# Two block products of seven parts in the output projection of a two-layer hybrid decoder trunk

## The chip, the cores and the metric

The kernel runs on one core of one Trainium2 chip. The metric is the device time in microseconds of one execution. The kernel before was run three times: 770.34, 770.36 and 770.64 us, median 770.36. Engines are called as the profile calls them: PE (TensorE matmul), PEld (its weight loads), DVE (VectorE), ACT (ScalarE), POOL (GpSimd), SP (SyncE, which here only issues DMAs).

## The reference

512 tokens and 16 learned meta tokens in front of them (528 in all) with 1024 features pass through two layers. All tensors are float32. Cut to what matters here, a layer computes:

```python
h = rmsnorm(h_res, norm_gain[l])
proj = h @ w_in[l]
u_pool, z_pool, c_q, c_kv, k_rope, z_mla, g_pool, g_mla = jnp.split(proj, IN_SPLIT_POINTS, axis=-1)
y_pool = (pool_mix(u_pool, ...) * jax.nn.silu(z_pool)) @ pool_w_up[l]
o_mla = mla(c_q, c_kv, k_rope, pos, ...)           # 8 heads, causal, latent queries and keys
y_mla = (o_mla * jax.nn.silu(z_mla)) @ mla_w_up[l]
merged = jax.nn.sigmoid(g_pool) * y_pool + jax.nn.sigmoid(g_mla) * y_mla
h_res = h_res + merged @ w_out[l]
```

After the second layer the meta tokens are dropped. The change is in the last line: `merged @ w_out[l]`, a product of 528 (in the second layer 512) tokens by 1024 by 1024.

## The kernel before, in words

Everything is held transposed: features lie on the 128 partitions, tokens along the free dimension. A product by a weight matrix is made output tile by output tile (128 features), over the tiles of the inner dimension K. To keep float32 accuracy, each operand is split into a high part rounded to float32r and a low part, the remainder, and each product is three matmuls in float32r, high by high, high by low and low by high (`mm3`, L181 to L183).

Weights come in chunks of four K tiles (128 x 512, 256 KB). `wload` (L170 to L178) fetches a chunk on SP's queue into one of three raw buffers, ACT rounds it to the high part `whi` (L176), DVE subtracts to get the low part `wlo` (L177). The high and low buffers rotate over three, or two, each.

The work is a plan of products (`Gemm`), filled by `register`, and one generator (`stream`) that emits them in order and loads one chunk ahead. `go` advances this generator and puts the other work (norm sums, pooling, heads) between its steps. This gives a program order with priorities; a scheduler then decides, from its own estimate of when each instruction is ready, the order in which each engine gets its instructions. On the chip each engine and each queue takes its instructions strictly in that order and waits on semaphores.

Tokens are worked in two halves of 264 in layer 0, and in one piece of 512 columns in layer 1, where meta tokens are no longer needed (its last output tile alone is made in two halves of 256). A PSUM buffer holds one tile of one such piece. There are four of the kind `mm` and three of the kind `S`.

The end of a layer runs through these products:

- mu0 to mu7, the MLA up-projection, four K tiles each. The evacuation `ev_mu` has DVE multiply PSUM with the gate (L980), POOL add the pool branch that lies in `xb[m]` (L982), and `split` round the sum on ACT into `hh[m]` (L275) and subtract on DVE into `hl[m]` (L276). These are the merged values, and the operand of the next product.
- o0 to o7, the output projection, eight K tiles each. The evacuation `ev_o` has DVE add the residual (L996), which SP fetched into a temporary tile, and store it. In layer 0 the result is the next layer's x, kept in `xb[m]`, squared on ACT and summed on POOL (`square_x`); in layer 1 it goes to the output `yT` (L1000).
- In layer 0, then, `split_h` of the next layer, which rounds x into the same `hh` and `hl` tiles that o0 to o7 read.

## Time and profile before

The profiled execution has a span of 768.5 us from the first to the last instruction. The execution's own time lies around that; the median of the runs, 770.36 us, is 1.86 us above the span.

| engine | busy, us | share of the span | instructions |
|---|---|---|---|
| PE | 763.8 | 99% | 5195 |
| PEld | 697.9 | 91% | 5195 |
| DVE | 544.1 | 71% | 1179 |
| ACT | 408.9 | 53% | 892 |
| POOL | 201.6 | 26% | 251 |

The granted PE clock is full (9 of 9 tenths) in all slices, and the DMA queues moved 84.05 MB, 109 GB/s on average.

How to read the profile's rows. A group of instructions is: line, engine, operation, output tile<-input tiles, shape, xcount | busy us, mean ns of one | idle time of the engine just before them, and what ended most of it. A row in order of time is: start us, duration us, engine, line, operation, tiles, shape, xcount [idle time before, and what ended it]. A row of the chain of work that ended last is: start, length, engine, tile, line. A row of waits is: who waited for whom, us in total, times, longest. A row of stretches is: stretch, its length, then the busy time of PE, PEld, DVE, ACT and POOL with counts, the granted clock, the share of the DMA engines' time and GB/s. A row of DMA issues ends in the size and the median time to landing. Durations of matmuls overlap, so the pace is read from starts.

### The profile page before, as it was taken

The page shows a single profiled execution, that of the slowest core. Times are in us where ns is not written, and L with a number is a line of the kernel's source. Part 1 is how long each engine was busy: PE and PEld are TensorE (multiplying, and loading weights), DVE is VectorE, ACT ScalarE, POOL GpSimd, SP SyncE. Part 2 cuts the span into 40 slices and gives each one's busy share as a digit, 9 for nine tenths or more (in the row PEclk, how much of TensorE's full clock was granted, in tenths as well). Part 3 has the DMA queues.
Part 4 walks back from the last instruction along what each step waited for, and adds up shares of the span by engine and source line. Part 5 has one row for each costly group of instructions (what it writes and reads, how often), then busy time and mean ns, then how long its engine had stood idle before and what let it go on. Part 6 is the DMA issues. An engine that isn't in the chain of part 4 may idle for free.

```text
span 768.5 us, 14355 instructions
## 1 busy us (share of the span) xinstructions
PE 763.8 (99%) x5195; PEld 697.9 (91%) x5195; DVE 544.1 (71%) x1179; ACT 408.9 (53%) x892; POOL 201.6 (26%) x251
## 2 busy tenths in 40 slices
PE   9999999999999999999999999999999999999998
PEld 9999999999999999999997898887888888888887
DVE  5588687357899977785376486773677989775842
ACT  6755656545556665634264355454446666664320
POOL 2026204012242233052220262040132434420500
PEclk9999999999999999999999999999999999999999
DMA  8533233343223222325642333334433332222372
GB/s 293 160 113 98 75 97 98 104 141 105 89 79 91 84 71 70 107 71 169 178 133 97 110 86 89 96 87 127 125 119 90 94 93 77 82 69 70 119 222 98
DMA packets 54931, 84.05 MB, mean 109 GB/s; under 512 B 10006, under 2 KB 18582, under 8 KB 54860
## 3 DMA queue, kind: packets, MB, share of 16 engines
q1 hardware_dynamic: 54716, 82.87, 35.6%
q8 instruction: 41, 0.67, 0.4%
q14 instruction: 30, 0.25, 0.1%
q10 hardware_dynamic: 144, 0.26, 0.1%
HBM read 76.69 MB, written 4.29 MB: 105 GB/s over the span
## 4 chain that ended last, share of the span: by engine, by line
PE 99%; DMA 0%; ACT 0%; DVE 0%; SPq 0%; issue 0%; ACTq 0%
PE mm L181 29%; PE mm L183 29%; PE mm L182 29%; PE mm L859 2%; PE S L181 2%; PE S L182 2%; PE S L183 2%; PE o L876 1%; PE o L872 1%; PE S L503 1%; PE S L470 0%; DMA xb<-xT 0%; PE S L806 0%; PE mm L922 0%; PE mm L395 0%; PE S L872 0%
## 5 line engine op out<-in xcount | busy, mean ns | idle before, releaser
L181 PE MATMUL mm<-hh,whi 128*128 128x264 f32 (+2 forms) x1080 | 339.9, 317 | 0.0
L182 PE MATMUL mm<-hl,whi 128*128 128x264 f32 (+2 forms) x1080 | 338.2, 314 | 0.0
L183 PE MATMUL mm<-hh,wlo 128*128 128x264 f32 (+2 forms) x1080 | 337.1, 315 | 0.0
L177 DVE TENSOR_TENSOR wlo<-raw,whi 128x512 fp32r<-128x512 f32 (+2 forms) x251 | 186.7, 748 | 98.6 <-ACT whi L176 94.6
L176 ACT ACTIVATE whi<-raw 128x512 fp32r<-128x512 f32 (+2 forms) x251 | 150.2, 602 | 181.3 <-PE mm L182 135.3
L181 PEld LDWEIGHTS mm<-hh,whi 128*128 128x128 f32 x1080 | 202.5, 188 | 12.9 <-ACT kp L474 0.4
L182 PEld LDWEIGHTS mm<-hl,whi 128*128 128x128 f32 x1080 | 203.0, 188 | 12.2
L183 PEld LDWEIGHTS mm<-hh,wlo 128*128 128x128 f32 x1080 | 201.9, 188 | 12.2
L743 POOL TENSOR_TENSOR tmp<-kp,bc 64x528 f32<-64x528 f32 x16 | 25.6, 1600 | 123.9 <-PE mm L183 70.0
L604 POOL TENSOR_TENSOR racc<-racc,tmp 128x264 f32<-128x264 f32 (+1 forms) x15 | 14.3, 956 | 133.1 <-ACT tmp L603 133.1
L832 POOL TENSOR_TENSOR pm<-pa,rs 128x16 f32<-128x16 f32 x32 | 9.1, 285 | 126.1 <-DVE rs L827 126.1
L982 POOL TENSOR_TENSOR tmp<-tmp,xb 128x264 f32<-128x264 f32 (+1 forms) x24 | 26.9, 1138 | 56.0 <-DVE tmp L980 55.9
L774 DVE CUSTOM_DVE_ANT_0 S<-S,maskw,nqs 128x400 f32<-128x400 f32 (+4 forms) x80 | 38.4, 499 | 4.4 <-PE S L183 4.0
L781 ACT ACTIVATE cq<-S,bia 128x400 f32<-128x400 f32 (+2 forms) x48 | 24.6, 516 | 27.1 <-DVE bia L774 18.1
L181 PE MATMUL mm<-u,whi 128*128 128x264 f32 (+1 forms) x108 | 34.7, 322 | 0.0
L181 PE MATMUL mm<-cq,whi 128*128 128x264 f32 (+1 forms) x108 | 34.7, 321 | 0.0
L183 PE MATMUL mm<-u,wlo 128*128 128x264 f32 (+1 forms) x108 | 34.7, 321 | 0.0
L183 PE MATMUL mm<-cq,wlo 128*128 128x264 f32 (+1 forms) x108 | 34.5, 321 | 0.0
L182 PE MATMUL mm<-cq,whi 128*128 128x264 f32 (+1 forms) x108 | 34.5, 321 | 0.0
L834 POOL TENSOR_TENSOR cq<-cq,rs 128x384 f32<-128x384 f32 (+1 forms) x32 | 32.8, 1024 | 0.0
L276 DVE TENSOR_TENSOR tl<-mm,th 128x384 fp32r<-128x384 f32 (+1 forms) x48 | 27.9, 596 | 5.0 <-ACT th L275 4.8
L275 ACT ACTIVATE th<-mm 128x384 fp32r<-128x384 f32 (+1 forms) x48 | 24.1, 523 | 10.2 <-PE mm L859 9.2
(270 smaller groups left out, 1378.6 us busy)
## 6 DMA issues: line engine op xcount, KB each, us to landing
raw<-win SPq DMA_DIRECT2D x143, 256.0 KB, 2.6
raw<-wout SPq DMA_DIRECT2D x32, 256.0 KB, 3.0
bc<-kdr SPq DMA_DIRECT2D x16, 264.0 KB, 3.6
raw<-wpu SPq DMA_DIRECT2D x16, 256.0 KB, 2.7
raw<-wmu SPq DMA_DIRECT2D x16, 256.0 KB, 2.7
raw<-wqb SPq DMA_DIRECT2D x12, 256.0 KB, 2.6
xb<-xT SPq DMA_DIRECT2D x8, 264.0 KB, 5.7
tmp<-xT SPq DMA_DIRECT2D x16, 132.0 KB, 3.4
```

Of the source, the lines that this page charges most:

```text
L176: act.activation(hi[:, :n], raw[:, :n], AF.Copy)
L177: dve.tensor_sub(lo[:, :n], raw[:, :n], hi[:, :n].bitcast(F32))
L181: first = pe.matmul(out, wh, xh, start=start, stop=False)
L182: pe.matmul(out, wh, xl, start=False, stop=False)
L183: newest[0] = pe.matmul(out, wl, xh, start=False, stop=stop)
L275: act.activation(hi[:, a:b], src, AF.Copy)
L276: return dve.tensor_sub(lo[:, a:b], src, hi[:, a:b].bitcast(F32))
L743: gp.tensor_mul(kf[r0:r0 + 64, :], self.kp[r0:r0 + 64, :], bc[r0:r0 + 64, :])]
L774: return dve.tensor_tensor_reduce(out=sv, in0=sv, in1=mask, scale=nqs[:, i, h:h + 1], scalar=3e38, op0=ALU.add, op1=ALU.min, accum_out=bia ...
L781: act.activation(pv, sv, AF.Exp, scale=-1.0, bias=bia[:, i:i + 1], accum_out=rs[:, c:c + 1])
L834: gp.tensor_mul(pt[i][:, NM:], pt[i][:, NM:], rs[:, i:i + 1].to_broadcast([P, n - NM]))
L982: gp.tensor_add(t[:, :b - a], t[:, :b - a], self.am[m][:, a:b])
```

## The change

In each layer o0 to o3 stay as they were. Tiles 4 to 7 become two pairs, (4, 5) and (6, 7). For a pair the weights form a 2 x 2 block matrix (two output tiles by two halves of K) and the merged values another (two halves of K by two halves of tokens, 264 or 256 columns each). Their product is formed by a scheme of seven block products in place of eight, each of four K tiles and three passes, 12 matmuls. It needs four sums of weight blocks and four sums of token blocks:

- weight sums, in DRAM buffers, made in the layer itself: SP copies four blocks per pair after `zp0`, and POOL issues DMAs that add further blocks to them (`weight_sums`, stages 1 to 3, after `zp3`, `cq5` and `qr1`);
- token sums (`combine_split`, 16 per layer, asked for after mu7): DVE adds or subtracts float32 blocks, ACT rounds the result to a high part, DVE takes the remainder. For that `ev_mu` now leaves the float32 sum in `xb[m]`; the buffers are those of the attention's values, keys and others that are free by then.

The loads of w_out go through a new function, `oload`, and run up to three chunks ahead in place of one (`deep`). It rotates over nine places for high and low parts, and uses three more raw buffers. For o1, o2 and o3 and for two of the seven parts of a pair, DVE's subtraction is replaced: ACT writes the negated high part into the low tile, and a DMA on POOL's queue adds the raw chunk to it.

The seven parts are accumulated in three PSUM tiles; after each part DVE adds what is there, times 0.5 or -0.5, to the residual row, which is now fetched as a whole ahead of the pair. One PSUM tile (B) goes on being accumulated over four parts, with such an add between any two of them. The x of o0 to o3 for the next layer moves from `xb[m]` to other tiles.

```diff
+PAIRS = (2, 3)
+PACE = 600.0
+DEEP = 2
+LOW = (3, 5)
...
+    def oload(j, src, by_dma):
+        if j % 2 == 1 and j > 5:
+            raw = slot(f"kn{j // 2 % 3}")
+        else:
+            raw = rawt()
+        fetch(src, 512, raw, sp)
+        kind = ("w", "t", "w", "cq0", "w", "cq2", "t", "q0", "q2")[j % 9]
...
+        act.activation(hi[:, :512], raw[:, :512], AF.Copy)
+        if by_dma:
+            act.activation(lo[:, :512], raw[:, :512], AF.Copy, scale=-1.0)
+            gp.dma_start(lo[:, :512].bitcast(F32), raw[:, :512], accum_op=ALU.add)
+        else:
+            dve.tensor_sub(lo[:, :512], raw[:, :512], hi[:, :512].bitcast(F32))
+        return hi, lo
...
+            if g_.operand is not None:
+                return g_.operand(c // 512)
+            if g_.deep:
+                j = (int(g_.name[1][1:]) * 2 + c // 512)
+                return oload(j, g_.src[:, c:c + 512], j > 1)
...
-            if i >= 3 and i + 1 < len(flat):
-                ahead.append(load(i + 1))
+            while made[0] < len(flat) and made[0] <= i + 1 + flat[made[0]][0].deep:
+                ahead.append(load(made[0]))
+                made[0] += 1
...
-                gp.tensor_add(t[:, :b - a], t[:, :b - a], self.am[m][:, a:b])
-                split(*self.mg[m], t[:, :b - a], a, b)
+                f = self.am[m][:, a:b]
+                gp.tensor_add(f, t[:, :b - a], f)
+                split(*self.mg[m], f, a, b)
...
+        def combine(self, w, k):
+            n = self.HV[0][1] - self.HV[0][0]
+            (a0, b0), (a1, b1) = self.HV
+            lo, hi = self.am[k], self.am[4 + k]
+            f = self.tf[w, k] = sqt()[:, :n]
+            eng = dve
+            if w == 1:
+                eng.tensor_sub(f, lo[:, a0:b0], lo[:, a1:b1])
+            elif w == 2:
+                eng.tensor_add(f, hi[:, a1:b1], self.tf[1, k])
+            elif w == 3:
+                eng.tensor_sub(f, hi[:, a1:b1], lo[:, a1:b1])
+            else:
+                eng.tensor_sub(f, self.tf[2, k], hi[:, a0:b0])
+
+        def combine_split(self, w, k):
+            self.combine(w, k)
...
+            sign = -1.0 if w == 2 else 1.0
+            act.activation(th, f, AF.Copy, scale=sign)
+            dve.scalar_tensor_tensor(out=tl, in0=f, scalar=sign, in1=th.bitcast(F32), op0=ALU.mult, op1=ALU.subtract)
+
+        def weight_sums(self, stage):
+            acc = lambda d, src: behind(gp.dma_start(d, src, accum_op=ALU.add, max_dma_last_dim=2048), newest[0])
+            for p in PAIRS:
+                w = lambda odd, c: wout[self.l, 2 * p + odd, :, 512 * c:512 * c + 512]
...
+                s1, s2, s3, s4 = self.ws[p]
+                if stage == 0:
+                    for d, src in ((s1, w(1, 0)), (s3, w(1, 0)), (s2, w(0, 0)), (s4, w(0, 1))):
+                        behind(sp.dma_start(d, src), newest[0])
+                elif stage == 1:
+                    acc(s1, w(1, 1))
+                    acc(s3, w(0, 0))
+                else:
+                    acc(*((s2, s1), (s4, s2))[stage - 2])
...
+                j = 4 * PAIRS[0] + 7 * (p - PAIRS[0]) + i
+                return oload(j, (raw(0, 0), raw(0, 1), s2, s1, s3, s4, raw(1, 1))[i], i in LOW)
...
+            def product(ps, w, xs, start):
+                for k in range(4):
+                    wh, wl = (x[:, k * P:(k + 1) * P] for x in w)
+                    xh, xl = xs[k]
+                    for j, (u, v) in enumerate(((wh, xh), (wh, xl), (wl, xh))):
+                        newest[0] = pe.matmul(ps, u, v, start=start and k == 0 and j == 0, stop=k == 3 and j == 2,
+                                              skip_group_check=not start)
...
+                if i == 0:
+                    product(B, w, quarter(0, a0, b0), True)
+                    add(m1, a0, b0, B, 0.5, False)
+                elif i == 1:
+                    product(A, w, quarter(4, a0, b0), True)
+                    add(m1, a0, b0, A, 0.5, True)
+                elif i == 2:
+                    product(B, w, ts(2), False)
+                    add(m1, a1, b1, B, 0.5, False)
...
-            for m in range(8):
-                add(f"o{m}", wout[l, m], D, evac=self.ev_o(m, nxt), xs=mg,
-                    segs=[(NM, NM + SEQ // 2), (NM + SEQ // 2, T)] if self.last and m == 7 else XS)
+            for m in range(2 * PAIRS[0]):
+                add(f"o{m}", wout[l, m], D, evac=self.ev_o(m, nxt), xs=mg, segs=XS)
+                plan[-1].deep = DEEP
...
+            for p in PAIRS:
+                add(f"o{2 * p + 1}", None, 7 * 512, body=self.pair_body(p, nxt))
+                plan[-1].operand, plan[-1].deep = self.pair_operand(p), DEEP
...
+            up("mu7")
+            flush()
+            for w in (1, 2, 3, 4):
+                for k in range(4):
+                    fill_now(PACE)
+                    self.combine_split(w, k)
             up("o7")
```

## The prediction

> **What bounds the kernel now.** I read the page's first part, then its chain of work, then stretches around the output projection, which is where the change sits.

> ```profile
> span 768.5 us, 14355 instructions
> PE 763.8 (99%) x5195; PEld 697.9 (91%) x5195; DVE 544.1 (71%) x1179; ACT 408.9 (53%) x892; POOL 201.6 (26%) x251
> PE 99%; DMA 0%; ACT 0%; DVE 0%; SPq 0%; issue 0%; ACTq 0%
> ```

> PE has no hole worth a word, and the chain that ended last is PE for 99% of its length. So a matmul taken away is time taken away, as long as nothing makes PE wait where it did not wait before. The last rows of the chain in time (765.13 below) are one add and one store, and they stay.

> The pace of a matmul is the step from start to start, not its own duration, because matmuls overlap:

> ```profile
> 346.07 0.29 PE L181 MATMUL mm<-hh,whi 128*128 128x264 f32 x1
> 347.54 0.28 PE L181 MATMUL mm<-hh,whi 128*128 128x264 f32 x1
> 351.81 0.28 PE L183 MATMUL S<-hh,wlo 128*128 128x264 f32 x1
> ...
> 720.38 0.39 PE L181 MATMUL mm<-hh,whi 128*128 128x512 f32 x1
> ...
> 754.63 0.39 PE L182 MATMUL mm<-hl,whi 128*128 128x512 f32 x1
> 759.02 0.40 PE L183 MATMUL mm<-hh,wlo 128*128 128x512 f32 x1
> 759.25 0.28 PE L181 MATMUL mm<-hh,whi 128*128 128x256 f32 x1
> ...
> 764.81 0.28 PE L183 MATMUL mm<-hh,wlo 128*128 128x256 f32 x1
> ```

> 346.07 to 351.81 is 47 steps, 0.122 us for 264 columns; 754.63 to 759.02 is 19 steps, 0.231 us for 512; 759.25 to 764.81 is 47 steps, 0.1183 us for 256. Also: the output projection of layer 0 starts at 346.07, its second half of tokens at 347.54, and that of layer 1 at 720.38. These are the handover points.

> VectorE at the handover from mu (the MLA up-projection) to o (the output projection), layer 0 then layer 1, as groups by form:

> ```profile
> L276 DVE TENSOR_TENSOR hl<-tmp,hh 128x264 fp32r<-128x264 f32 x16 | 11.3, 720 | 1.2 <-ACT hh L275 1.2
> L177 DVE TENSOR_TENSOR wlo<-raw,whi 128x512 fp32r<-128x512 f32 x7 | 5.5, 801 | 0.1
> L980 DVE SCALAR_TENSOR_TENSOR tmp<-cq,mm 128x264 f32<-128x264 f32 x12 | 4.8, 421 | 3.2 <-PE mm L183 3.0
> L982 POOL TENSOR_TENSOR tmp<-tmp,xb 128x264 f32<-128x264 f32 x16 | 14.6, 927 | 27.8 <-DVE tmp L980 27.6
> L176 ACT ACTIVATE whi<-raw 128x512 fp32r<-128x512 f32 x7 | 4.3, 622 | 4.5 <-PE mm L182 3.9 <-DMA raw<-wout 0.6
> ...
> L177 DVE TENSOR_TENSOR wlo<-raw,whi 128x512 fp32r<-128x512 f32 x10 | 10.2, 1032 | 0.9 <-ACT whi L176 0.9
> L276 DVE TENSOR_TENSOR hl<-tmp,hh 128x512 fp32r<-128x512 f32 x8 | 7.1, 905 | 1.1 <-ACT hh L275 1.1
> ```

> And the instructions themselves, in order of time (start, duration):

> ```profile
> 345.12 0.43 DVE L980 SCALAR_TENSOR_TENSOR tmp<-cq,mm 128x264 f32<-128x264 f32 x1
> 346.75 0.42 DVE L980 SCALAR_TENSOR_TENSOR tmp<-cq,mm 128x264 f32<-128x264 f32 x1
> 348.61 0.42 DVE L980 SCALAR_TENSOR_TENSOR tmp<-cq,mm 128x264 f32<-128x264 f32 x1
> 348.94 0.42 DVE L276 TENSOR_TENSOR hl<-tmp,hh 128x264 fp32r<-128x264 f32 x1
> 349.29 0.42 DVE L980 SCALAR_TENSOR_TENSOR tmp<-cq,mm 128x264 f32<-128x264 f32 x1
> ...
> 708.07 1.28 DVE L980 SCALAR_TENSOR_TENSOR tmp<-cq,mm 128x512 f32<-128x512 f32 x2 [2.86 <-PE mm L183]
> 721.71 1.87 DVE L980 SCALAR_TENSOR_TENSOR tmp<-cq,mm 128x512 f32<-128x512 f32 x3
> ```

> The idle columns are small after the first wait: VectorE is full there. An evacuation of mu6 runs at 346.75 and ends at 347.17; the matmul at 347.54 reuses that PSUM buffer. The margin is 0.37 us. VectorE's 71% over the whole span hides that it is within half a microsecond of being the bound at this place.

> **The change, part by part.**

> *Matmuls.* Of each layer the tiles 4 to 7 go from eight block products to seven. Layer 0 drops 24 matmuls of 264 columns: 24 x 0.122 = 2.93 us. Layer 1 drops 72 of 512 (16.63) and 24 x 2 = 48 of 256, and gets 168 of 256, so +120 x 0.1183 = 14.20: 2.44 us gained. Together -5.37 us, all on the path.

> *Token sums.* Per layer 16 VectorE sums, 16 ScalarE roundings, 16 VectorE remainders. The kernel's text asks for them after mu7, but in the changed program's instruction order they stand between the evacuations of mu, because their inputs are ready from mu0 on. Ahead of the mu6 evacuation named above stand nine token instructions that were not there, and two splits (hl) less; the weight subtractions (wlo) are five in both. One token instruction costs at least the step 348.61 to 348.94 to 349.29, 0.35 us, and at most what hl takes on average beside POOL, 0.72 less 0.08 of overlap, 0.64. A gain is excluded, since nothing is removed from that queue but the two splits. Seven net: 2.45 to 4.5 us. POOL's adds fill 14.6 of about 22 us, so I take 0.35 + 0.29 x 0.66 = 0.54, 3.8 us; less the margin, PE stands still 3.4 us (2.1 to 4.1) at the first o tile of layer 0.

> [...]

> *Layer 1.* From 708.07 on, VectorE must do, ahead of the remainder of the last mu tile: 8 evacuations (1.87/3 = 0.62) 5.0, 6 wlo (1.03 - 0.08) 5.7, 8 hl (0.905 - 0.08) 6.6, and 23 token instructions, 8.1 to 14.7, by 0.54 12.4. That is 25.4 to 32.0, taken as 29.7, so it is done at 737.8. PE needs it after 67 matmuls of its new order (60 of 512, 7 of 256): 720.38 + 14.7 = 735.1. Stall 2.7 us (0 to 4.6).

> *Weight parts.* 22 instead of 16 loads of w_out per layer: 6 x 0.62 on ACT more, and 10 negated copies, 6.2 us; VectorE's subtractions fall from 16 to 12. Ten low parts come from accumulating DMAs on POOL's queue. No row shows one. The nearest is a plain load of the same 256 KB:

> ```profile
> raw<-wout SPq DMA_DIRECT2D x32, 256.0 KB, 3.0
> ACT whi L176 <- PE mm L182: 135.3, 103, 3.9
> 346.00:392.00 46.00, 46.00 (x379) 46.00 (x379) 22.62 (x41) 17.86 (x32) 8.47 (x8) 1.00 0.59 174
> 765.13 0.42 DVE tmp L996
> 765.58 0.33 SPq L1000 DMA_DIRECT2D yT<-tmp  x1
> ```

> It reads one operand more, so 3.0 is the low end and 6.0, twice, the high one; I take 3.4, near the row, plus 0.9 on POOL to issue (its own add, 0.927; 0.3 as on SP would be the low end). Queued behind such a DMA on POOL are the last mu adds, behind their ScalarE copies the last roundings of mu, and behind them on SP the next load, which waits for the raw buffer that the DMA still reads. In layer 0: the fourth wlo of the stretch frees a raw buffer near 341.6, 12 us after the first evacuation by the counts above; its load takes 3.0 and three ScalarE items 0.62 each, so the copy for o1's second half ends near 346.4. Then +0.9 +3.4, the load that waits for that buffer +3.0, four ScalarE items 2.6: the last mu rounding ends at 356.3. PE wants it 58 matmuls in, 353.1, and with the 3.4 us it already stood still, 356.5: hidden, barely. Without that cover it is a stall of 3.2. In layer 1 the DMA for o1 starts behind the fifth mu add, near 720.5, and lands at 724.8 against 724.1; the load that reuses its buffer lands at 727.8, two ScalarE items and two issues on POOL later the DMA for o2 starts at 730.1 and lands at 733.5 against 731.6. Both hide under the 2.7.

> [...]

> *Sums of weights.* Per layer eight DRAM copies on SP in a row behind a zp matmul (8 x 0.33 = 2.6 us of SP) and eight accumulates on POOL. By 174 GB/s at a share of 0.59 the engines carry some 295 GB/s, so the 2.1 MB delay the next weight loads by about 7 us. The cover is the 135.3 us in which ScalarE waited for PE to release a weight buffer: loads stand two to three 2.9 us chunks ahead. Nothing, 0 to 3 us if that runs out. POOL's rope products and the last c_q sum wait behind accumulates by a few us; head 0 is some 30 us later.

> *Pair stage.* A part is 12 matmuls, 1.46 us. Per pair of 10.2 us VectorE has 5 wlo (0.69) and 7 adds (0.43), 6.5 us; ScalarE 9 x 0.62. The shared PSUM buffer is read by an add before the next part continues into it; in the new order some 20 matmuls, 2.4 us, lie between. Nothing; 16 x 0.43 if they touch. The DMA share of 0.59 rises by 6 loads and 10 accumulates: 16 to 26 times 256 KB at 295 GB/s, 14 to 23 of 46 us, to 0.9 or 1.1. Nothing at the low end.

> *The rest.* mu's sum is written in place (same add), the next layer's x moves to other buffers, residual rows load earlier, the last store is again 256 columns wide behind one add (765.13): nothing.

> Sum against the span: 768.5 - 5.37 + 3.4 + 2.7 = 769.2. The median of the runs, 770.36, is 1.86 above this execution's span: **771.1 us**. About 0.2% (1.5 us) is what a measurement of this kernel can tell from no change.

> **The rivals.**

> *Handover mostly holds (faster).* If a token instruction costs its bare 0.35 us, layer 0 stalls 2.1 and layer 1 not at all: 25.4 after 708.07 is 733.5, before 735.1. Sum -3.3: 767.1. For it: POOL's adds are a fixed amount of work, so their collisions need not grow with VectorE's. Against it: hl at 720 ns against 420 alone. It decides below about 0.45 us.

> *Accumulating DMAs bind (slower).* At 4.5 us each, layer 0's chain ends at 357.4 against 353.1, a stall of 4.3; in layer 1 the low part of o2 waits for two accumulates and a load in series, 736.0 against 731.6, 4.4: 773.7. At 6.0 us, 5.8 and 6.9: 777.7. I price it at 775.5. It decides from about 3.7 us. For it: the second read, and a DMA share near 1. Against it: loads on all 16 engines land in 3.0 with a share of 0.59.

> *It is hidden anyway.* If PE finds other work while a PSUM buffer is late: 765.0. Against it: PE takes its matmuls in the order written, and that order was set before any wait was known.

> **How the numbers follow.** Forecast, 0.38, own range 768.3 to 773: mostly inside 0.2%, a quarter slower. Handover holds, 0.33. DMAs bind, 0.25. Hidden, 0.04. Faster 0.30 + 0.04 + 0.03 = 0.37; the same 0.25 + 0.03 = 0.28; slower 0.35. The range 766.3 to 777.0 leaves out the hidden case and the worst DMAs, and because cases of both signs hold most of the chance it is wider than the forecast's own.

> **What would show it.** PE gaps at two places: the second half of o0 in layer 0, released by a VectorE evacuation, and near the last mu tile's remainder in layer 1. VectorE without idle from mu0 to o0, token instructions at 0.5 to 0.6 us. If PE's gaps are ended by a POOL-queue DMA instead, or landing takes over 4 us, the DMA rival holds. No gap anywhere and a PE time near 758 means it is hidden. I am wrong most simply if the gaps sit in the pair stage or behind the DRAM copies.

## The result, and the profile after

The changed kernel takes 784.63 us (median of four runs, 781.7 to 784.91) against 770.35: ratio 1.0173, 95% interval 1.0153 to 1.0192. The prediction was 771.1, range 766.3 to 777.0: the result lies outside it, on the slow side of every case in it (the slowest, DMAs of 6.0 us, gave 777.7). The profiled execution spans 782.8 us, 14.3 more than before.

The head of the page of the changed kernel, and its chain of work that ended last:

```profile
span 782.8 us, 14643 instructions
PE 767.4 (98%) x5219; PEld 699.5 (89%) x5219; DVE 571.8 (73%) x1250; ACT 433.5 (55%) x956; POOL 230.2 (29%) x287
...
PE 81%; DMA 10%; DVE 5%; issue 2%; ACT 1%; SPq 1%; POOL 0%; DVEq 0%; ACTq 0%; POOLq 0%
```

PE was 99% of the chain and is now 81%; a tenth of the chain is waiting for DMAs. PE's busy time went up although it has less to multiply, a first hint that some matmuls ran slower; the clock below shows it. PE's instructions in order of time, only those that waited longest (in brackets: the idle time and what ended it):

```profile
105.14 0.36 PE L208 MATMUL mm<-hh,whi 128*128 128x264 f32 x1 [0.61 <-DVE xb L585]
132.49 0.39 PE L210 MATMUL mm<-cq,wlo 128*128 128x264 f32 x1 [0.29 <-DVE wlo L179]
...
350.12 0.39 PE L208 MATMUL mm<-hh,whi 128*128 128x264 f32 x1 [2.03 <-DVE tmp L1016]
...
493.85 0.50 PE L208 MATMUL mm<-hh,whi 128*128 128x512 f32 x1 [0.32 <-ACT whi L178]
...
730.00 0.50 PE L208 MATMUL mm<-hh,whi 128*128 128x512 f32 x1 [0.44 <-DVE tmp L1016]
734.12 0.50 PE L210 MATMUL mm<-hh,tl 128*128 128x512 f32 x1 [1.07 <-DVE tl L199]
737.98 0.50 PE L209 MATMUL mm<-hl,th 128*128 128x512 f32 x1 [1.50 <-DVE hl L309]
...
762.32 0.80 PE L1099 MATMUL mm<-vt,th 128*128 128x256 f32 x2 [3.84 <-DVE bc L1105]
```

Such gaps lie in three parts of the program: the stretch where the weights are summed (near 100 to 130 and 490 to 530 us), the handovers from mu to o (350 and 730 to 741), and the pair stage of layer 1 (762). Two of them leave something behind. Stretches of the same kernel:

```profile
348.14:351.56 3.42, 1.45 (x12) 1.45 (x12) 3.42 (x5) 2.29 (x7) 2.17 (x3) 1.00 0.69 144
351.56:354.97 3.41, 3.31 (x16) 3.00 (x15) 3.41 (x8) 1.75 (x4) 2.27 (x3) 0.50 0.64 108
757.74:761.16 3.42, 0.74 (x7) 0.54 (x5) 0.52 (x1) 2.19 (x4) 0.60 (x1) 1.00 0.62 236
761.16:767.99 6.83, 5.67 (x26) 5.67 (x27) 3.81 (x9) 1.78 (x3) 1.13 (x2) 0.50 0.61 135
740.00:760.00 20.00, 18.21 (x97) 15.04 (x96) 11.95 (x28) 11.61 (x25) 3.34 (x4) 1.00 0.99 289
```

After each of the two long gaps the granted clock (the figure before the DMA share) is at half, once for 3.41 us and once for 6.83. And before the second one the DMA engines are full: 0.99 at 289 GB/s. The kernel before is some 10 us further in its program at the same time, so the stretch to compare is its 730 to 750 us, about the same work, with 0.74 at 227 GB/s:

```profile
730.00:750.00 20.00, 20.00 (x88) 16.21 (x87) 8.53 (x13) 5.06 (x8) 0.00 (x0) 1.00 0.74 227
```

Where the time went, worked out from the starts of all matmuls: the step from each to the next, less the usual step of its shape, added up by part of the program, after minus before, in us:

| part | lost | of it the clock |
|---|---|---|
| sums of weights, both layers | 2.9 | 0 |
| handover of layer 0, and 0.4 in its pair stage | 5.3 | 1.7 |
| handover of layer 1 | 4.8 | 0 |
| pair stage of layer 1 | 6.6 | 2.8 |
| sum | 19.6 | 4.5 |

768.5 - 5.4 (the dropped matmuls, an estimate from their pace) + 19.6 is 782.7, against a span of 782.8: no larger loss is left out. The clock's part is an estimate, half of the time that PE worked at half clock, 3.31 / 2 and 5.67 / 2 by the rows above. Measured from start to start, 264 columns took 0.220 us there in place of 0.122 and 256 columns 0.213 in place of 0.118; added up over the two stretches, that and the slower steps at their beginnings are 1.8 and 2.6 us.

### The profile page after: what moved, and what is told of

The parts are those of the page before. It is cut to its first block, busy times and chain, and to the rows that moved or that the text cites. A ratio compares the mean times of both kernels' runs of the same rounds, so it can differ in the third digit from the quotient of the medians.

```text
span 782.8 us, 14643 instructions
## 1 busy us (share of the span) xinstructions
PE 767.4 (98%) x5219; PEld 699.5 (89%) x5219; DVE 571.8 (73%) x1250; ACT 433.5 (55%) x956; POOL 230.2 (29%) x287
## 3 DMA queue, kind: packets, MB, share of 16 engines
q1 hardware_dynamic: 58460, 90.22, 35.9%
q0 software_dynamic: 5184, 9.44, 7.4%
## 4 chain that ended last, share of the span: by engine, by line
PE 81%; DMA 10%; DVE 5%; issue 2%; ACT 1%; SPq 1%; POOL 0%; DVEq 0%; ACTq 0%; POOLq 0%
PE mm L208 22%; PE mm L210 22%; PE mm L209 21%; PE mm L1099 4%; PE mm L895 2%; DMA raw<-wout 2%; PE S L208 2%; PE S L209 2%; PE S L210 2%; DVE wlo L179 2%; DMA raw<-wqb 2%; DMA raw<-wgr 1%; PE o L912 1%; PE o L908 1%; DMA tmp<-xT 1%
## 5 line engine op out<-in xcount | busy, mean ns | idle before, releaser
L208 PE MATMUL mm<-hh,whi 128*128 128x264 f32 (+1 forms) x924 | 292.1, 318 | 3.5 <-DVE tmp L1016 2.5
L209 PE MATMUL mm<-hl,whi 128*128 128x264 f32 (+1 forms) x924 | 289.8, 315 | 0.0
L210 PE MATMUL mm<-hh,wlo 128*128 128x264 f32 (+1 forms) x924 | 288.8, 316 | 0.0
L179 DVE TENSOR_TENSOR wlo<-raw,whi 128x512 fp32r<-128x512 f32 (+2 forms) x219 | 164.5, 754 | 80.7 <-ACT whi L178 76.6
L178 ACT ACTIVATE whi<-raw 128x512 fp32r<-128x512 f32 (+2 forms) x219 | 130.0, 598 | 141.7 <-PE mm L209 78.2
L208 PEld LDWEIGHTS mm<-hh,whi 128*128 128x128 f32 x924 | 174.0, 189 | 15.6 <-DVE tmp L1016 3.4
L209 PEld LDWEIGHTS mm<-hl,whi 128*128 128x128 f32 x924 | 174.3, 189 | 10.3 <-DVE hl L309 0.2
L210 PEld LDWEIGHTS mm<-hh,wlo 128*128 128x128 f32 x924 | 173.1, 189 | 10.7 <-DVE wlo L179 0.3
L1019 POOL TENSOR_TENSOR xb<-tmp,xb 128x264 f32<-128x264 f32 (+1 forms) x24 | 27.3, 1166 | 52.6 <-DVE tmp L1016 52.6
L308 ACT ACTIVATE th<-mm 128x384 fp32r<-128x384 f32 (+1 forms) x48 | 24.1, 523 | 10.2 <-PE mm L895 9.2
## 6 DMA issues: line engine op xcount, KB each, us to landing
raw<-win SPq DMA_DIRECT2D x143, 256.0 KB, 2.6
raw<-wout SPq DMA_DIRECT2D x20, 256.0 KB, 2.7
ws<-wout SPq DMA_DIRECT2D x16, 256.0 KB, 5.0
raw<-wpu SPq DMA_DIRECT2D x16, 256.0 KB, 2.8
raw<-wmu SPq DMA_DIRECT2D x16, 256.0 KB, 2.6
raw<-wqb SPq DMA_DIRECT2D x12, 256.0 KB, 4.6
```

The lines of the kernel that those rows point to most:

```text
L178: act.activation(hi[:, :n], raw[:, :n], AF.Copy)
L179: eng.tensor_sub(lo[:, :n], raw[:, :n], hi[:, :n].bitcast(F32))
L208: first = pe.matmul(out, wh, xh, start=start, stop=False)
L209: pe.matmul(out, wh, xl, start=False, stop=False)
L210: newest[0] = pe.matmul(out, wl, xh, start=False, stop=stop)
L1019: gp.tensor_add(f, t[:, :b - a], f)
```

## The experiments

They run from what adds one part to the kernel before, over what takes one part out of the change, to all parts at once. Before them, the rows of the changed kernel that the theories rest on. Its queues and engines in order of time, first at the sums of weights (SP, ACT), then VectorE and POOL at the handovers, then SP and VectorE in the last pair stage:

```profile
97.48 0.53 SPq L118 DMA_DIRECT2D raw<-wgr  x1
102.24 0.31 ACT L178 ACTIVATE whi<-raw 128x128 fp32r<-128x128 f32 x1 [3.05 <-DMA raw<-wgr]
...
347.93 1.79 DVE L1032 TENSOR_TENSOR sq<-xb,sq 128x264 f32<-128x264 f32 x1
349.65 0.41 DVE L1016 SCALAR_TENSOR_TENSOR tmp<-cq,mm 128x264 f32<-128x264 f32 x1
...
730.47 3.59 DVE L199 TENSOR_TENSOR tl<-raw,th 128x512 fp32r<-128x512 f32 x1
730.64 2.87 POOL L1019 TENSOR_TENSOR xb<-tmp,xb 128x512 f32<-128x512 f32 x2
...
754.74 0.32 SPq L1153 DMA_DIRECT2D tmp<-scr  x1
760.64 0.69 DVE L1160 SCALAR_TENSOR_TENSOR tmp<-mm,tmp 128x512 f32<-128x512 f32 x1 [4.57 <-DMA kn<-wout]
```

A load of 64 KB, issued right behind the eight copies, lands 4.7 us later (the median of these loads is 1.8), and ACT stands for it; VectorE's next subtraction stands behind ACT, and the evacuation that ends PE's gap at 105.14 stands behind that in VectorE's queue. A token sum of 264 columns takes 1.79 us, a subtraction of 512 columns 3.59, in each case beside POOL's adds. And the evacuation of o3 stands 4.6 us. The row names a weight load (`kn<-wout`) as what ended that wait, but the instruction doesn't read this tile; what it reads is its residual row, `tmp<-scr`, issued at 754.74 and landed near 760.45.

**The sums of weights alone (e1_sums_alone).** The kernel before, plus the copies and accumulating DMAs; their result is unused.

```diff
             self.mix(2, s2)
+            self.weight_sums(0)
...
+            up("zp3")
+            self.weight_sums(1)
             up("cq5")
+            self.weight_sums(2)
...
+            self.weight_sums(3)
```

> The kernel before, with only the sums of weights added (the eight DRAM copies and eight accumulating DMAs per layer; nothing reads their result). Theory (the lost time has three separate sources, of which the sums are one): by the PE gaps that the changed kernel has near 104, 132, 493 and 510 to 530 us, the time rises by 0.9 + 0.6 + 0.9 + 0.5 = 2.9 us, to 773.2 (772.5 to 774.0), with PE gaps at the same places and ended by the same instructions. Rival (my prediction: the loads ahead of PE cover the copies, and those gaps come from another part of the change): 770.4, no gap.

Measured: 774.56 us, ratio 1.0047 (1.0033 to 1.0062), so 2.5 to 4.8 us. Its PE waits are in the expected places, in layer 0 only in this execution:

```profile
105.61 0.36 PE L182 MATMUL mm<-hh,whi 128*128 128x264 f32 x1 [1.11 <-DVE xb L551]
121.92 0.39 PE L182 MATMUL mm<-cq,whi 128*128 128x264 f32 x1 [0.47 <-ACT tmp L605]
```

The sums cost by themselves. "Nothing" is refuted. The times fall in two groups, near 773.1 and 775.8, and the execution profiled, at 772.74, is of the faster one; what divides them was not found.

**Low parts on VectorE (e2_low_on_dve).** No accumulating DMA for low parts.

```diff
-LOW = (3, 5)
+LOW = ()
...
-                return oload(j, g_.src[:, c:c + 512], j > 1)
+                return oload(j, g_.src[:, c:c + 512], False)
```

> The changed kernel with all low parts of w_out made by a subtraction on VectorE, none by an accumulating DMA. Theory (accumulating DMAs are not what binds): the gap at the handover in layer 0 stays or grows, since up to three more subtractions stand in VectorE's queue there; the time stays within 780 to 787 us. Rival (the accumulating DMAs bind, by their landing time of 4 to 6 us and by filling the DMA engines): at least 5 us faster than the changed kernel, 779.5 or less, with the gaps of layer 1 gone.

Measured: 780.07, ratio 1.0118 (1.0103 to 1.0134): 4.6 us faster than the change, although VectorE has 20 subtractions more. The time is just inside the theory's 780 to 787 and misses the rival's 779.5, so neither held whole. The gap near 758 us is gone, and that at layer 0's handover is 1.52 us, where the theory had it stay or grow: the accumulating DMAs do cost, though not alone. Two other gaps took their place, of 3.0 us in layer 0's pair stage, ended by an add, and of 2.0 in layer 1, ended by a subtraction on VectorE:

```profile
381.77 0.48 PE L1099 MATMUL mm<-vt,th 128*128 128x264 f32 x2 [3.00 <-DVE bc L1105]
...
740.04 0.50 PE L210 MATMUL mm<-hh,wlo 128*128 128x512 f32 x1 [2.04 <-DVE wlo L199]
```

**No token sums (e3_no_token_sums).** The pairs multiply plain quarters of the merged values.

```diff
-                ts = lambda w_: [self.ts[w_, k] for k in range(4)]
+                ts = lambda w_: quarter(4 * (w_ % 2), a1, b1)
...
-            for w in (1, 2, 3, 4):
-                for k in range(4):
-                    fill_now(PACE)
-                    self.combine_split(w, k)
```

> The changed kernel without the 16 token sums per layer: the seven-part products take plain quarters of the merged values instead, so the output of tiles 4 to 7 is not the reference's; all matmuls and all weight parts stay. Theory (VectorE's queue makes the gaps at the handover): both handovers lose their gaps, 2.2 us and the 1.7 us at half PE clock behind it in layer 0, 0.8 + 3.2 + 0.8 in layer 1, some 9 us; the late residual row near 758 us and the half clock behind it stay: 775.5 (774 to 777). Rival (the gaps there come from the DMAs and from POOL's adds, the token sums only fill VectorE): 781 or more.

Measured: 777.86, ratio 1.0080 (1.0058 to 1.0103), between the two; the four runs spread from 775.56 to 780.76, and the profile is of the slowest. In it the wait at the handover of layer 0 falls from 2.03 to 0.28 us: that one is the token sums'. Layer 1 keeps gaps of 1.35 and 1.11 us, ended by a low and a high part of weights: there weight parts are late by themselves. The wait near 760 us shrank to 0.68, and one of 1.92 us came in the pair stage of layer 0, neither of which the theory had expected.

**Residual rows early (e4_residual_early).** Issued ahead of the weights of o0 to o3, into buffers of their own.

```diff
+            if self.last:
+                self.xr[m] = slot(f"cq{8 + m}")
+                sp.dma_start(self.xr[m][:, self.x0:T], scr[:, m, :])
```

> The changed kernel with the residual rows of o0 to o3 in layer 1 loaded into four buffers of their own, ahead of the weights of their tile, in place of the three shared temporaries. Theory (the 4.0 us gap near 758 us is VectorE waiting in its queue for o3's residual row, whose load stood on SP behind the store that frees its buffer): the gap goes and with it the 2.6 us at half PE clock: 778.0 (777 to 780). Rival (the DMA engines are full in that stretch, share 0.99, and whatever is late there only changes its name): 782 to 785, with a new gap ended by a weight part.

Measured: 786.56, ratio 1.0204 (1.0167 to 1.0241), with runs from 783.29 to 790.08. The theory fell: the residual row is there, and a gap of 3.17 us is too. It was the rival in kind, though the time lies above its 782 to 785 as well. ACT and VectorE at that place, in order of time, and SP's waits from 720 us on:

```profile
760.25 0.63 ACT L194 ACTIVATE q<-raw 128x512 fp32r<-128x512 f32 x1 [4.56 <-DMA raw<-wout]
760.91 0.69 DVE L199 TENSOR_TENSOR q<-raw,q 128x512 fp32r<-128x512 f32 x1 [3.81 <-ACT q L194]
```

```profile
SPq L118 <- DMA wlo<-kn: 4.9, 2, 3.2
SPq L118 <- DMA cq<-raw: 4.3, 2, 3.2
```

What is late is now a weight load. Ahead of it SP stood in its queue 3.2 us for a buffer that an accumulating DMA was still reading, and then it took over 5 us to land. The new theory: SP takes its loads in order, one load that waits for such a buffer holds every load, store and residual row behind it, and what PE then waits for is only the first of them to be needed. The changed kernel shows the same (SP's waits, 340 to 400 us, then 720 to 782):

```profile
SPq L118 <- DMA cq<-raw: 9.7, 2, 5.5
SPq L118 <- DMA wlo<-raw: 7.6, 3, 3.8
```

```profile
SPq L118 <- DMA wlo<-raw: 4.6, 2, 2.9
SPq L118 <- DMA cq<-raw: 3.4, 2, 3.1
```

From 720 us on, this view also has longer waits of SP's stores for VectorE's adds, 10.4 us in the longest line; they begin when the last weight load has been issued, so they hold none.

**Token sums held back (e5_tokens_held).** A dependency that only orders VectorE's queue.

```diff
-PACE = 600.0
+PACE = 1000.0
...
-                eng.tensor_sub(f, lo[:, a0:b0], lo[:, a1:b1])
+                held = eng.tensor_sub(f, lo[:, a0:b0], lo[:, a1:b1])
...
+            follow(held, newest[0])
```

> The changed kernel with each token sum held back, in the order of VectorE's queue alone, behind the matmul of o0 to o3 that PE is then at (one sum per us), so that none stands among the evacuations of mu. Theory (VectorE's queue makes the gaps at both handovers): they go, 2.2 + 1.7 + 0.7 us in layer 0 and 0.8 + 3.2 + 0.8 in layer 1, and the late load near 758 us stays: 775 (773.5 to 778). Rival (the sums cost as much wherever they stand, since the pairs then wait for them): 781 or more, with gaps ended by the remainder of a token sum.

Measured: 779.54, ratio 1.0111 (1.0092 to 1.0129), between the two ranges. The wait at layer 0's handover is 0.18 us and no clock is lost there, as expected; layer 1's keeps gaps of 1.21 and 0.98 us, ended by weight parts. Less is gained than the gaps promised, since a later one comes forward:

```profile
379.55 0.48 PE L1100 MATMUL mm<-vt,th 128*128 128x264 f32 x2 [2.57 <-DVE bc L1106]
```

**Sums of weights in the heads (e6_sums_in_heads).** One of the eight stages behind each attention head.

```diff
                 kn_ = self.head(h, kq, prev)
+                self.weight_sums(h)
                 self.gap()
```

> The changed kernel with the sums of weights spread over the eight attention heads (one copy per pair behind each of the heads 0 to 3, one accumulating DMA per pair behind each of the heads 4 to 7) in place of the stretch from zp0 to qr1. Theory (it is the burst that makes the weight loads late, not the sums as such; the DMA share in the heads is 0.25 to 0.33): the gaps near 104, 132, 493 and 510 to 530 us go, and with them what the sums alone cost in the kernel before, 4.0 us: 780.6 (779.5 to 782). Rival (the price moves along with the transfers): 784 to 786, with gaps among the heads.

Measured: 780.68, ratio 1.0128 (1.0104 to 1.0151), as expected. No PE gap over 0.3 us is left between 10 and 340 us, nor from 390 to 720: the same bytes leave no gap where the DMA engines are else a quarter to a third busy (0.23 to 0.32 in the kernel before, from 180 to 300 us).

**All three (e7_all_three).** The edits of the runs e2, e5 and e6 together:

```diff
-LOW = (3, 5)
+LOW = ()
...
+            follow(held, newest[0])
...
+                self.weight_sums(h)
```

> The changed kernel with all three edits: token sums held back, sums of weights spread over the heads, low parts of w_out by subtractions on VectorE. Theory (three separate sources, and they add: 9.4 us by the gaps of the handovers, 4.0 by the sums alone, 4.5 by the low parts on VectorE): 766.7 (765 to 770), so no slower than the kernel before. Rival (the pair stage binds by itself: its loads, stores and residual rows stand in one queue on SP, and VectorE has 12 + 14 + 32 instructions more there): 772 to 778, with the gaps in the stretches 365 to 400 and 740 to 770 us.

Measured: 769.98, ratio 0.9991 (0.9981 to 1.0001), at the slow end of the theory's range. One by one the edits gain 4.6, 5.1 and 3.9 us, 13.6 together; all at once, 14.7. In time they are close to additive, though one by one each let another gap grow, and what remains equals the kernel before.

**A repeated evacuation (e8_stall_8).** The kernel before, with mu6's first evacuation done nine times, meant to open a gap of 2.4 us.

```diff
+                for _ in range(8 + 1 if (self.l, m, a) == (0, 6, 0) else 1):
                     dve.scalar_tensor_tensor(out=t[:, :b - a], ...
```

> The kernel before, with one evacuation (mu6, first half of the tokens, layer 0) done nine times in place of once, so that PE waits there for VectorE: 8 x 0.35 less the margin of 0.37 us is a stall of 2.4 us. Theory (a stall of about 2 us also takes PE's clock to half for a while, as in the rows of the changed kernel near 352 us, 3.4 us at half speed): 2.4 + 1.7 = 4.1 us, 774.5, with a stretch of granted clock 0.5 behind the gap. Rival (a stall costs its own length and no more): 772.8 and clock 1.0 throughout.

Measured: 772.12, ratio 1.0015 (1.0004 to 1.0025). The repeats came to stand spread among other work on VectorE, and the longest wait was 0.58 us, so this says nothing on the clock.

**Low parts by DMA again (e9_low_by_dma), and for o1 and o2 alone (e10_dma_o1_o2).** From the kernel with all three edits, the first with the change's own `LOW` and `j > 1`, the second with

```diff
-                return oload(j, g_.src[:, c:c + 512], False)
+                return oload(j, g_.src[:, c:c + 512], 2 <= j < 6)
```

> The kernel of the run before with all three edits (769.98 us), but with the low parts made by accumulating DMAs again, as the change has them: token sums held back, sums of weights in the heads. Theory (an accumulating DMA has a price of its own: it still reads the raw buffer 4 to 6 us after its issue, and SP, which takes its loads in order, waits for that buffer): 774.5 (773 to 776), with gaps in the pair stages ended by weight parts or by an add behind one. Rival (the price came only from meeting the late VectorE and the burst of sums): 771 or less.

> The kernel with all three edits (769.98 us), with accumulating DMAs for the low parts of o1 and o2 alone, whose subtractions stand among the last evacuations of mu. Theory (what they take off VectorE at the handover, four subtractions of 0.6 us, they give back by the raw buffers that they hold): 769.5 to 771.5. Rival (only VectorE's queue counts at the handover): its gaps of 0.5, 0.6, 0.7 and 0.6 us go, 768.0 or less.

Measured: 775.16, ratio 1.0078 (1.0049 to 1.0106), and 773.83, ratio 1.0037 (1.0024 to 1.0051). The DMAs have a price of their own, 5.2 us for all 20 by the medians (the five runs spread from 774.16 to 780.52), and it is there without the burst of sums and without token sums among the evacuations of mu. Even the eight DMAs at the handover, where they take work off a full VectorE, cost 3.8 us more than they give, above both expectations. The runs also bear out the theory of SP's queue: from 340 to 400 us SP waits for no accumulating DMA in the kernel with all three edits, and in the first run (SP's waits) its longest line is the first row below. A wait of SP is no loss by itself: in the kernel before SP waits 21.2 us in that stretch for VectorE's subtractions, and PE never stands. In the second run PE waits for an accumulating DMA directly, the second row:

```profile
SPq L118 <- DMA wlo<-raw: 14.4, 4, 6.0
...
736.50 0.50 PE L210 MATMUL mm<-hh,wlo 128*128 128x512 f32 x1 [1.08 <-DMA wlo<-raw]
```

**Low parts held back too (e11_low_held).**

```diff
-            dve.tensor_sub(lo[:, :512], raw[:, :512], hi[:, :512].bitcast(F32))
+            follow(dve.tensor_sub(lo[:, :512], raw[:, :512], hi[:, :512].bitcast(F32)), newest[0])
```

> The kernel with all three edits (769.98 us), with the subtractions for the low parts of w_out also held back, in the order of VectorE's queue, behind the matmul that PE is at, three chunks ahead of their use. Theory (the gaps left at the handovers are evacuations and remainders of mu behind work that PE doesn't need yet): 0.5 + 0.6 + 0.7 + 0.6 us go, 767.6 (767 to 769). Rival (the subtractions then come late for PE, or hold the raw buffers and with them SP): 770 or more, with gaps ended by low parts.

Measured: 774.27, ratio 1.0053 (1.0036 to 1.0069): the rival. No PE gap over 0.3 us is left at layer 0's handover, but from 373 to 390 us five stand, four of them new, of 0.5 to 1.6 us, three ended by weight parts.

**The last adds of mu on VectorE (e12_mu_adds_dve).** From the kernel with all three edits.

```diff
-                gp.tensor_add(f, t[:, :b - a], f)
+                (dve if m >= 4 else gp).tensor_add(f, t[:, :b - a], f)
```

> The kernel with all three edits (769.98 us), with the adds of mu4 to mu7 on VectorE in place of POOL. Theory (while POOL adds, a VectorE instruction with two inputs in SBUF stands still: subtractions of 0.68 us take 1.24 to 1.79 us there): VectorE gets 8 x 0.35 us in layer 0 and 4 x 0.6 us in layer 1 more, and loses about as much standing still: 769 to 770.5, and its subtractions of 128x512 take 0.7 us throughout. Rival (VectorE's own number of instructions is what counts, POOL does not slow it): 772 or more.

Measured: 766.95 (766.37 to 768.79), ratio 0.9956 (0.9941 to 0.9971): faster than the kernel before, the changed one and the one with three edits, and by more than expected. Its busy times:

```profile
PE 759.7 (99%) x5219; PEld 695.7 (91%) x5219; DVE 576.7 (75%) x1282; ACT 425.5 (56%) x936; POOL 201.4 (26%) x255
```

More work on VectorE, less waiting for it: no wait at the handovers is over 0.2 us, and the longest anywhere behind the first 10 us is 0.8.

**The same edit to the changed kernel (f1_change_mu_adds_dve) and to the kernel before (f2_before_mu_adds_dve).** In the latter:

```diff
-                gp.tensor_add(t[:, :b - a], t[:, :b - a], self.am[m][:, a:b])
+                (dve if m >= 4 else gp).tensor_add(t[:, :b - a], t[:, :b - a], self.am[m][:, a:b])
```

> The changed kernel with one edit: the adds of mu4 to mu7 on VectorE in place of POOL. Theory (at the handovers VectorE mostly stands still behind POOL's adds, as in the rows where a subtraction of 0.68 us takes 1.78 and 3.59 us): the gaps there shrink although VectorE gets 2.8 us (layer 0) and 2.4 us (layer 1) of instructions more; 779.5 (777 to 781.5). Rival (the number of VectorE's instructions makes the gaps, as the prediction had it): they grow, 785 or more.

> The kernel before with the same edit, as a control. Theory (PE has no gap there that VectorE ends, so nothing can be gained): 770.4, within 0.2%, and the 766.95 of the run with all edits is the dropped matmuls showing. Rival (the adds on POOL cost the kernel before as well): 768.5 or less.

The control: 771.34, ratio 1.0008 (0.9999 to 1.0017). The edit by itself gains nothing, so the 766.95 is best read as the dropped matmuls showing. The changed kernel with it: 787.64, ratio 1.0220 (1.0203 to 1.0238), slower, as the rival had it, but not for the rival's reason. Groups on VectorE by form around layer 0's handover, the changed kernel (329 to 352 us), then this one (346 to 358):

```profile
L309 DVE TENSOR_TENSOR hl<-xb,hh 128x264 fp32r<-128x264 f32 x11 | 7.4, 677 | 0.0
...
L1030 DVE TENSOR_TENSOR sq<-xb 128x264 f32<-128x264 f32 x4 | 2.7, 677 | 0.0
L1050 DVE SCALAR_TENSOR_TENSOR vt<-sq,vt 128x264 fp32r<-128x264 f32 x4 | 2.5, 623 | 0.0
...
L1032 DVE TENSOR_TENSOR sq<-xb,sq 128x264 f32<-128x264 f32 x1 | 1.8, 1789 | 0.0
```

```profile
L1050 DVE SCALAR_TENSOR_TENSOR vt<-sq,vt 128x264 fp32r<-128x264 f32 x3 | 1.3, 428 | 0.0
L1032 DVE TENSOR_TENSOR sq<-xb,sq 128x264 f32<-128x264 f32 x3 | 1.3, 423 | 0.0
```

Without POOL's adds a token instruction takes 0.42 us, beside them 0.62 to 1.79, and the gap behind the evacuation is gone. Its place takes the next thing that is late; ACT and PE of this run in order of time:

```profile
355.56 0.63 ACT L194 ACTIVATE th<-raw 128x512 fp32r<-128x512 f32 x1 [3.37 <-DMA raw<-wout]
361.62 0.59 PE L208 MATMUL mm<-hh,th 128*128 128x264 f32 x1 [3.12 <-ACT hh L308]
```

The last roundings of mu stand on ACT behind the rounding of a weight chunk whose load waited on SP, 3.9 us, for a buffer under an accumulating DMA. This chain was in the prediction, as hidden. The longest gap of this run, in layer 1, is ended by an accumulating DMA itself:

```profile
744.46 0.79 PE L210 MATMUL mm<-hh,wlo 128*128 128x512 f32 x1 [3.75 <-DMA wlo<-raw]
```

**A PE gap of set length (f3_gap_short, f4_gap_long).** The kernel before; the matmuls of zp2 wait for 4 or 16 memsets on the idle POOL.

```diff
+    def hold():
+        hs = cp.tile([P, 256], F32, name="hs")
+        for i in range(16):
+            held[0] = gp.memset(hs, 0.0)
+            behind(held[0], newest[0])
...
+        if held[0]:
+            for ins in (first, second, newest[0]):
+                behind(ins, held[0])
```

> The kernel before with one PE gap put in: the matmuls of zp2 in layer 0 wait for four memsets of 128x256 on the idle POOL that start behind the last matmul of zp1, some 1.4 us. Theory (a 3.4 us stretch that is idle for under about half leaves the clock as it is): the gap's own length and no more, 771.9 (771.3 to 772.4), clock 1.0. Rival (any gap costs clock): 773.5 or more.

> The same with sixteen memsets, some 4.6 us. Theory (a stretch of the 3.4 us grid that is idle for over half takes the clock to half for the next one, and a cold stretch costs half its length): 4.6 + 1.7 = 6.3 us, 776.8, or 4.6 + 3.4 where two stretches are hit, 778.5, with granted clock 0.5 behind the gap. Rival (a gap costs its own length only): 775.1, clock 1.0.

Measured: 771.98, ratio 1.0018 (1.0008 to 1.0028), and 779.09, ratio 1.0110 (1.0095 to 1.0125). PE's gap in the first, PE's gap in the second, and the second's stretches around it:

```profile
99.09 0.39 PE L181 MATMUL mm<-hh,whi 128*128 128x264 f32 x1 [1.54 <-POOL hs L194]
```

```profile
103.78 0.59 PE L181 MATMUL mm<-hh,whi 128*128 128x264 f32 x1 [5.96 <-POOL hs L194]
```

```profile
99.60:103.00 3.40, 0.00 (x0) 0.00 (x0) 2.84 (x10) 1.38 (x3) 2.88 (x10) 1.00 0.33 96
103.00:109.84 6.84, 6.06 (x27) 6.06 (x28) 0.32 (x1) 0.54 (x1) 0.62 (x2) 0.50 0.00 0
```

The short gap costs 1.4 us, no more than its length. The long one came out at 6.0 in place of 4.6, and costs 8.5 (8.9 in the execution profiled): 2.5 to 2.9 more than its length, with two stretches at half clock (at 0.22 us from start to start in place of 0.122, the 6.06 us that PE worked in them lose 2.7, an estimate from these paces). This long gap cost more than itself.

## Why the prediction was wrong, step by step

*Sums of weights, "nothing, 0 to 3": the first step that failed.* Alone they cost 3.6 us (2.5 to 4.8), in the changed kernel 2.9. The cover, 135.3 us of ACT waiting for PE, was a total over the whole span; in the 33 us in question, 92 to 125, ACT waited for PE to release such a buffer for 3.3 us only (the row below, of the kernel before), and in the changed kernel a load behind the eight copies landed 4.7 us after its issue. The text named the DRAM copies as the simplest way to be wrong, and gave them no chance.

```profile
ACT whi L176 <- PE mm L182: 3.3, 5, 1.1
```

*Pair stage, "nothing": the second.* It lost 6.6 us in layer 1. The forecast that the DMA share would reach 0.9 to 1.1 nearly came true (0.88 in layer 0's 350 to 396 us, 0.99 in layer 1's 740 to 760); to price that at the low end was the mistake. Beside that share o3's residual row took 5.7 us to land, and the loads all stand in one queue.

*Accumulating DMAs, 3.4 us and hidden: the third.* Issues by line of the changed kernel (KB each, us to landing):

```profile
wlo<-raw POOLq DMA_DIRECT2D x8, 256.0 KB, 4.0
cq<-raw POOLq DMA_DIRECT2D x4, 256.0 KB, 5.4
wlo<-kn POOLq DMA_DIRECT2D x4, 256.0 KB, 5.3
tl<-raw POOLq DMA_DIRECT2D x2, 256.0 KB, 5.9
```

The rival that they bind (chance 0.25, from 3.7 us on) was right in the landing time and in the two chains, but not in where they show: the chain in layer 0 that was "hidden, barely" and the one in layer 1 come out as the gaps of 3.12 and 3.75 us only once VectorE no longer stands in front (the run with the adds of mu on VectorE). At 4.5 to 6.0 us it gave 773.7 to 777.7, and with the two other sources taken out the kernel stands at 775.16; that this lies between is partly luck, since the gaps of that run lie in the pair stages and in layer 1's handover. In this company the DMAs for low parts took 4.0 to 5.9 us to land (medians of the rows above), the plain loads of w_out and of its sums, of the same size, 2.7 to 5.1; the packets of POOL's queue took 7.4% of the DMA engines' time for 9.44 MB, those of SP's 35.9% for 90.22 MB. That a second read is the reason was the author's estimate, and is not shown.

*Token sums at layer 0's handover, 3.4 us (2.1 to 4.1): right in mechanism, and in size at the low end.* The gap is 2.03 us (2.2 by the starts), ended by VectorE's L1016, at the first o matmul. That is the evacuation of mu6's first half, with eight token instructions ahead of it; the prediction had named that of the second half, which has nine ahead, as counted. A token instruction was taken at 0.54 us net; from mu0's first evacuation to mu6's last one VectorE now takes 351.58 - 331.27 = 20.31 us in place of 346.75 - 329.42 = 17.33, so the seven instructions net cost 2.98, 0.43 each. Their own durations are longer: the groups above give (2.7 + 2.5 + 1.8) / 9 less 0.08 of overlap, 0.70. Both hold, since POOL's adds are the same work as before, and part of the standing still moved to the tokens from hl, whose mean fell from 0.76 us (the row below, the kernel before from 329 to 347.2 us) to 0.68 (the groups above).

```profile
L276 DVE TENSOR_TENSOR hl<-tmp,hh 128x264 fp32r<-128x264 f32 x12 | 8.9, 762 | 0.2 <-ACT hh L275 0.2
```

So in layer 0 the rival "Handover mostly holds" was the nearer one, with its argument, its limit of 0.45 us and its stall of 2.1 us; its 767.1 left out the other sources. The durations depend on POOL by the traces: in the changed kernel the subtractions of 264 columns into hl took 0.43 us where POOL ran nothing and 0.66 on average where it did (0.42 to 0.99), the evacuations of the same width from PSUM 0.42 in both, and in the run with the adds on VectorE a token instruction took 0.42.

*Layer 1's handover, 2.7 us (0 to 4.6).* It lost 4.8, and only partly as described: without token sums gaps of 1.35 and 1.11 us stay, behind weight parts. (The upper end was also summed too low: 708.07 + 32.0 less 735.1 is 5.0.) How the 4.8 divides between token sums, POOL's adds and late weight parts stays open.

*Clock, not in the sum at all.* Some 4.5 us of the 19.6 lost. The trace of before has no gap behind its first us and no half clock; the prediction treated a stall as costing its length.

*Matmuls, -5.37 us: nothing against it.* The table above closes with it, and with the sources removed the kernel is 3.6 us faster than before.

So the mechanisms were nearly all named, but three of them were set at nothing behind a cover that was not there where it was needed. 19.6 us were lost where 6.1 were forecast.

## What to carry to other kernels

A cover counts only in the stretch where it is needed: take waits and DMA share by window, not from a total over the span. Here accumulating DMAs kept their raw buffers for 4.0 to 5.9 us, SP stood up to 5.5 us for one of them and issued nothing from 357.4 to 363.0 us, and what is seen to be late may not be what is wrong: moving the late residual row earlier gained nothing (786.56 us against 784.63). When PE is the bound, put bulk transfers where the DMA engines have room (3.9 us here), and hold back work that is ready early but needed late; holding back the subtractions that PE needs within a few us cost 4.3 us. Moving adds from POOL to VectorE gained 3.0 us where nothing else was late, nothing in the kernel before, and lost 3.0 where accumulating DMAs were: try such an edit on the kernel that it is meant for.

## What was not expected of the hardware

One VectorE subtraction of 512 columns took 3.59 us in place of 0.68 while POOL did two adds.
